# Weights of a float32 layer: rounded by the transfer, low parts made by a negative copy and an adding transfer

## The chip, the cores and the metric

The kernel runs on one core of a Trainium2 chip. The metric is the time of one execution on the device in microseconds (us). The engines that matter here are TensorE (PE: matmuls; its weight loads are listed as PEld), VectorE (DVE), ScalarE (ACT), GpSimd (POOL), which does almost no arithmetic here but issues some transfers, and SyncE (SP), which issues the rest. Every engine works through its own instructions in order.

## The reference

One decoder layer on 512 tokens of width 1024, all float32. Cut to what matters:

```python
h = rmsnorm(x, norm_mix_g)
proj = h @ w_in            # qk_ml, v_ml, o_ml, if, q_sw, k_sw, v_sw, g_a, g_b
h_ml = mlstm_chunkwise(q_ml, k_ml, v_ml, ig, lf)      # 4 heads
y_a  = sigmoid(o_ml) * norm(h_ml) * mlstm_norm_g
y_b  = swa_with_sinks(q_sw, k_sw, v_sw, sinks)        # window 128, 16 heads on 4
merged = sigmoid(g_a) * (y_a @ w_branch_a) + sigmoid(g_b) * (y_b @ w_branch_b)
x = x + merged @ w_out
x = x + square(relu(rmsnorm(x, norm_mlp_g) @ w_up)) @ w_down       # 1024 -> 4096 -> 1024
x = x + sigmoid(rmsnorm(x, norm_ple_g) @ w_ple_gate) * (p @ w_ple_proj)
return rmsnorm(x, final_norm_g)
```

The result must be right to float32 accuracy.

## The kernel before

**Products.** TensorE multiplies numbers of a rounded type, float32r. Each float32 operand is therefore split in two, a high part (the value rounded to float32r) and a low part (what is left, value − high), and a product is three matmuls: high·high, high·low, low·high (`pairs`, L154; the matmul itself is L162). 128 x 128 blocks of one operand are held, up to 512 columns of the other stream past.

**Weight tiles.** Weights lie in HBM as tiles of 128 partitions x 1024 values, 512 KB. SP loads a raw tile into a buffer `wr` (`load_raw`, L141; the load is L143), ACT rounds it into `wh` (L134), and DVE subtracts `wh` from the raw values into `wl` (L135). There are four buffers of each kind (`WRB` = 4 and `WB` = 4), so a raw tile is loaded while earlier ones are still at work. With one tile of `w_o`, `w_up` and the like, TensorE makes 24 matmuls of 512 columns (8 blocks x 3). `w_vsif` alone has two tiles of 1056 (4 x 264).

**Schemes of seven half products.** The value projection (`w_vml`), the two gates (`w_gb`, `w_ga`) and the down projection of the MLP (`w_down`) are written by Strassen-like schemes: seven products of half-sized blocks for eight. There DVE adds and subtracts raw weight tiles first, and the sums are split; each such tile feeds 12 matmuls of 512 columns or 24 of 256.

**Order of the work.** normalisation of x and `w_vsif` with it; `w_ksw` (2 tiles); `w_o` (8, among mLSTM gate arithmetic); the value scheme; the gates' schemes; then `w_qsw` and `w_qkml` (8 each), laid between the units of sliding-window attention; the mLSTM with `w_b` (8) between its heads; `w_a` (8); `w_out` (8); four rounds of up (8 tiles of `w_up`) and down (a scheme of 14 products); the projection of p (`w_pp`, 2); the gate projection (`w_pg`). `w_pg` is done in two halves: four tiles one after the other, each for all tokens, into four banks (psp); then, from L1073, four tiles that are all used for every 256 columns of every group of 128 tokens (psg), so that all four are needed within the first 48 matmuls. `gate` (L1029 to L1034) evicts: a sigmoid on ACT, a product and a sum on DVE, a square on ACT.

The tile framework puts each engine's instructions in an order of its own making when the program is built, and a buffer is reused when its last reader is through. POOL's queue held 16 stores of intermediate results to DRAM (`god<-sgo`, `gd<-gr`), 8 additions (L803) and the constants of the start.

Of the kernel before, what the change touches and what calls it, by code (L numbers as in the profile page):

```python
# [10 lines left out]
F32 = mybir.dt.float32  # L11
F32R = mybir.dt.float32r
AF = mybir.ActivationFunctionType
# [23 lines left out]
def block_kernel(  # L37
# [48 lines left out]
    def nm(s):  # L86
        n_names[0] += 1
        return f"{s}_{n_names[0]}"
# [50 lines left out]


    def load_raw(src, n):  # L141
        raw = wp.tile([P, 1056], F32, tag="wr", bufs=WRB, name=nm("wr"))
        nc.sync.dma_start(out=raw[:, :n], in_=src)  # L143
        return raw

    def load_w(src, n, dims, raw=None):

        if raw is None:
            raw = load_raw(src, n)
        parts = [wp.tile([P, 1056], F32R, tag=t, bufs=WB, name=nm(t))[:, :n] for t in ("wh", "wl")]  # L150
        split(parts, raw[:, :n])
        return [q.rearrange("p (k c) -> p k c", k=dims) for q in parts]

    def pairs(a, b):  # L154

# [8 lines left out]
    def quads(src, tags):  # L164

        t = []
        for i in range(len(tags)):
            if tags[i] == "wr":
                raw = wp.tile([P, 1056], F32, tag="wr", bufs=WRB, name=nm("wr"))[:, :1024]
            else:  # L170
                raw = sp.tile([P, 1024], F32, tag=tags[i], bufs=LMB if tags[i] == "lm" else 2, name=nm("wq"))
            nc.sync.dma_start(out=raw, in_=src[i])
            t.append(raw)
        return t
# [8 lines left out]
    def mm_tok(ps, w, acts, m, first=True, last=True):  # L183

        ops = []
        for k in range(len(acts)):
            ops += pairs([q[:, m * P : (m + 1) * P] for q in acts[k]], [q[:, k, :] for q in w])
        chain(ps, ops, first, last)
# [39 lines left out]
    nc.sync.dma_start(out=grow, in_=g_mix)  # L228
    load_x(0, 2)
    load_x(1)  # L230
    wv = [load_raw(w_vsif[c], 4 * 264) for c in range(2)]
    load_x(2)
    load_x(3)
    gml = cols(g_ml, KT, "gml", c1)
# [30 lines left out]
    for m in range(NT):  # L265
        xn = tok_scratch("xn")
        ss = small("ss", 1)
        A.activation(xn, xt[m], AF.Square, accum_out=ss)
        rs = rstd_of(ss, D)
        for c in range(2):  # L270
            o = slice(c * 512, (c + 1) * 512)
            V.scalar_tensor_tensor(xn[:, o], xt[m][:, o], rs, gmix[:, o], ALU.mult, ALU.mult)
        xns.append(xn)
        if m == 0:
            wv = [load_w(None, 4 * 264, 4, wv[c]) for c in range(2)]

    vs = []
    gt = c1.tile([P, NT, 8], F32, name="gt")
# [2 lines left out]
    for m in range(NT):  # L281
        for kq in range(2):
            ps = ps_t()
            for k in range(4):
                T.transpose(ps[:, k * P : (k + 1) * P], xns[m][:, kq * 512 + k * P : kq * 512 + (k + 1) * P], ident)
            split(
                [t[:, 4 * kq : 4 * kq + 4, m * P : (m + 1) * P] for t in h2],
                ps.rearrange("p (k c) -> p k c", k=4),
            )

        ps = ps_g()
        for c in range(2):
            mm_tok(ps[:, :264], wv[c], hT[c * 4 : c * 4 + 4], m, first=c == 0, last=c == 1)
        t = sp.tile([P, 256], F32, tag="vs", bufs=4, name=nm("vs"))
        A.copy(t, ps[:, :256])
        gate_in = V.tensor_add(gt[:, m, :], ps[:, 256:264], bif)
        vs.append(t)
# [576 lines left out]
    def load_down(q):  # L874
        raws = []
        for c in range(8):
            if c < 6:
                t = np_.tile([P, 1024], F32, tag="wd", bufs=6, name=nm("wd"))
            else:
                t = wp.tile([P, 1056], F32, tag="wr", bufs=WRB, name=nm("wr"))[:, :1024]  # L880
            nc.sync.dma_start(out=t, in_=w_down[q * 8 + c])
            raws.append(t)
        return raws

    def up(q, uf):
        fs = None
        for f in range(8):
            ps = ps_g()
            mm_T(ps, load_w(w_up[q * 8 + f], KT * P, KT), x1)
            a = mp.tile([P, 512], F32, tag="rt", bufs=3, name=nm("rt"))  # L890
            V.scalar_tensor_tensor(a, ps, 0.0, rB, ALU.max, ALU.mult)  # L891
            if f % 2 == 0:
                fs = F()
            o = 2 * (f % 2)
            A.activation(fs[:, o : o + 2, :].rearrange("p a b -> p (a b)"), a, AF.Square)
            if f % 2:
                hl = [np_.tile([P, 7 * 256], F32R, tag="uf", bufs=8, name=nm("uf")) for _ in range(2)]

                cut = 3 * 256 if f == 7 else 0
                if cut:  # L900
                    split([t[:, :cut] for t in hl], fs[:, 1:4, :].rearrange("p a b -> p (a b)"))
                V.tensor_add(fs[:, S1, :], fs[:, A21, :], fs[:, A22, :])
                V.tensor_sub(fs[:, S3, :], fs[:, A11, :], fs[:, A21, :])
                V.tensor_sub(fs[:, S2, :], fs[:, S1, :], fs[:, A11, :])
                V.tensor_sub(fs[:, S4, :], fs[:, A12, :], fs[:, S2, :])  # L905
                split([t[:, cut:] for t in hl], fs[:, 1 + cut // 256 :, :].rearrange("p a b -> p (a b)"))
                uf.append(hl)
# [221 lines left out]
def _layout(i):  # L1129
    w = i["w_in"][0]  # L1130
    down = i["w_down"][0]
    return {
        "x": i["x"][0],
        "p": i["p"][0, 0],
        "w_qkml": _t_form(w[:, 0:1024]),
        "w_vml": _quarters(w[:, 1024:2048]).reshape(2, 4, P, 1024).transpose(1, 0, 2, 3).reshape(8, P, 1024),
        "w_o": _t_form(w[:, 2048:3072]),
        "w_vsif": _tok_form(np.concatenate([w[:, 4360:4616], w[:, 3072:3080]], axis=1), 4, 264),
        "w_qsw": _t_form(_heads(w[:, 3080:4104])),
        "w_ksw": _t_form(w[:, 4104:4360]),  # L1140
        "w_ga": _halves(w[:, 4616:5640]),
        "w_gb": _halves(w[:, 5640:6664]),
        "w_a": _t_form(i["w_branch_a"][0]),
        "w_b": _t_form(_heads(i["w_branch_b"][0].T).T),
        "w_out": _tok_form(i["w_out"][0], 2, 512),
        "w_up": _t_form(i["w_up"][0]),
        "w_down": np.concatenate([_quarters(down[q * 1024 : (q + 1) * 1024]) for q in range(4)], axis=0),
        "w_pg": _tok_form(i["w_ple_gate"][0], 2, 512),
        "w_pp": _tok_form(i["w_ple_proj"][0], 2, 512),
        "g_mix": i["norm_mix_g"],  # L1150
        "g_ml": _columns(i["mlstm_norm_g"][0]),
        "g_mlp": _columns(i["norm_mlp_g"][0]),
        "g_ple": _columns(i["norm_ple_g"][0]),
        "g_fin": i["final_norm_g"][None, :],
        "conv": i["conv_qk"][0].reshape(4, KT, P).transpose(2, 1, 0).reshape(P, KT * 4),
        "b_if": i["b_if"],
        "sinks": i["sinks"],
    }
# [19 lines left out]
```

## Time and profile before

| | us |
|---|---|
| median of 3 runs | 921.12 (921.03 to 921.82) |
| profiled execution, span | 919.4 |
| PE busy | 903.5 (98%) |
| DVE busy | 646.0 (70%) |
| ACT busy | 448.5 (49%) |
| POOL busy | 23.4 (3%) |

The runs lie 1.7 us above the span of the profiled execution. In the profile a row of a group gives the line of the kernel, the engine, the operation, output tile <- input tiles with their shapes, the count, then the busy time, the mean duration of one in nanoseconds, and the engine's idle time before these instructions with what ended it. In the timeline a row is: start, duration, engine, line, operation, tiles, count, and in brackets the idle time before with its releaser. A row of the transfers: destination <- source, the queue, the count, KB each, and the median time in us from issue to landing. A row of the windows: the stretch, its length, then busy time (and number of instructions) of PE, PEld, DVE, ACT and POOL, the granted TensorE clock, the share of the transfer engines, GB/s. The rows themselves stand in the prediction.

### The profile page before, as it was taken

To read this page: it belongs to the slowest core of one execution; us is meant where nothing else is said; L and a number is where in the kernel's file an instruction comes from. 1 tells how busy PE (TensorE), PEld (TensorE's weight loads), DVE (VectorE), ACT (ScalarE), POOL (GpSimd) and SP (SyncE) were. 2 spreads that over 40 slices of the span, in tenths; PEclk is the share of its full clock that TensorE was granted. 3 is DMA by queue.
4 is the path that set the end of the run, shared out by engine and by line. 5 is a ranking of instruction groups with operands and counts; after the bars stand their busy time and mean duration, and the time that the engine had idled before them with its cause. 6 is when DMAs were issued, how large, how long until landed. Compare 5 with 4: busy or idle time off the path is not lost.

```text
span 919.4 us, 11810 instructions
## 1 busy us (share of the span) xinstructions
PE 903.5 (98%) x4524; PEld 743.6 (81%) x4524; DVE 646.0 (70%) x1026; ACT 448.5 (49%) x756; POOL 23.4 (3%) x41
## 2 busy tenths in 40 slices
PE   8999999999999999999999999999999999999996
PEld 6877889998777676778888888888888888888886
DVE  5776677874787877467653578757966895798556
ACT  6364444443676667564322545334434433454743
POOL 1001000000000000000210000000000000000000
PEclk9999999999999999999999999999999999999998
DMA  6643124434211132233452520631162044102302
GB/s 240 216 142 126 58 73 163 169 118 167 69 60 56 46 115 70 73 110 138 160 184 92 206 91 1 204 117 46 65 209 94 1 159 143 65 24 72 135 1 92
DMA packets 29851, 100.46 MB, mean 109 GB/s; under 512 B 4193, under 2 KB 4705, under 8 KB 29794
## 3 DMA queue, kind: packets, MB, share of 16 engines
q1 hardware_dynamic: 28002, 93.41, 29.6%
q0 software_dynamic: 1792, 6.29, 1.9%
q8 instruction: 35, 0.57, 0.3%
q14 instruction: 22, 0.18, 0.1%
HBM read 90.26 MB, written 8.39 MB: 107 GB/s over the span
## 4 chain that ended last, share of the span: by engine, by line
PE 74%; ACT 3%; DVE 2%; issue 0%; ACTq 0%
PE psg L162 41%; PE psp L162 23%; PE pst L736 2%; PE pst L663 1%; PE psa L655 1%; PE pst L726 1%; PE psa L162 1%; PE psa L618 1%; PE psp L829 1%; PE psa L619 1%; ACT jk L748 1%; ACT pT L657 0%; DVE it L1047 0%; PE psa L705 0%; ACT sgp L1034 0%
## 5 line engine op out<-in xcount | busy, mean ns | idle before, releaser
L134 ACT CAST wh<-wr 128x1024 fp32r<-128x1024 f32 (+1 forms) x136 | 142.4, 1050 | 211.5 <-PE psg L162 92.9
L135 DVE TENSOR_TENSOR wl<-wr,wh 128x1024 fp32r<-128x1024 f32 (+1 forms) x136 | 173.6, 1279 | 98.0 <-ACT wh L134 98.0
L162 PE MATMUL psg<-x,wh 128*128 128x512 f32 x512 | 159.9, 393 | 0.0
L162 PE MATMUL psp<-wh,uf 128*128 128x512 f32 x448 | 140.7, 393 | 0.0
L162 PEld LDWEIGHTS psg<-x,wh 128*128 128x128 f32 x512 | 96.3, 188 | 21.0
L162 PE MATMUL psg<-h,wh 128*128 128x512 f32 x320 | 101.8, 397 | 0.0
L162 PE MATMUL psg<-x,wl 128*128 128x512 f32 x256 | 100.5, 392 | 0.0
L162 PEld LDWEIGHTS psp<-wh,uf 128*128 128x128 f32 x448 | 84.1, 188 | 18.8
L162 PE MATMUL psp<-wl,uf 128*128 128x512 f32 x224 | 88.0, 393 | 0.0
L134 ACT CAST wh<-wd 128x1024 fp32r<-128x1024 f32 x44 | 46.2, 1052 | 60.7 <-PE psp L162 27.5
L162 PEld LDWEIGHTS psg<-h,wh 128*128 128x128 f32 x320 | 58.8, 188 | 16.2 <-issue 4.9
L162 PE MATMUL psg<-h,wl 128*128 128x512 f32 x160 | 63.2, 395 | 0.0
L135 DVE TENSOR_TENSOR wl<-wd,wh 128x1024 fp32r<-128x1024 f32 x44 | 53.6, 1221 | 5.2 <-ACT wh L134 5.2
L162 PEld LDWEIGHTS psg<-x,wl 128*128 128x128 f32 x256 | 48.1, 188 | 10.6
L162 PE MATMUL psa<-h,wh 128*128 128x256 f32 (+1 forms) x256 | 55.2, 312 | 0.6 <-ACT p L543 0.4
L162 PEld LDWEIGHTS psp<-wl,uf 128*128 128x128 f32 x224 | 42.1, 188 | 9.5
L135 DVE TENSOR_TENSOR uf<-F,uf 128x1792 fp32r<-128x1792 f32 (+2 forms) x20 | 33.0, 1651 | 21.8 <-ACT uf L134 21.8
L162 PEld LDWEIGHTS psa<-h,wh 128*128 128x128 f32 x256 | 41.6, 189 | 4.6 <-ACT p L543 1.3
L162 PE MATMUL psg<-yb,wh 128*128 128x512 f32 x128 | 42.6, 409 | 0.0
L891 DVE SCALAR_TENSOR_TENSOR rt<-psg,rB 128x512 f32<-128x512 f32 x32 | 22.0, 688 | 27.9 <-PE psg L162 27.9
L162 PE MATMUL psg<-ya,wh 128*128 128x512 f32 x128 | 40.8, 396 | 0.0
L134 ACT CAST uf<-F 128x1792 fp32r<-128x1792 f32 (+2 forms) x20 | 27.9, 1396 | 26.1 <-DVE F L905 26.0
(272 smaller groups left out, 1683.8 us busy)
## 6 DMA issues: line engine op xcount, KB each, us to landing
wr<-in_w_up SPq DMA_DIRECT2D x32, 512.0 KB, 3.3
wd<-in_w_down SPq DMA_DIRECT2D x24, 512.0 KB, 3.5
wr<-in_w_o SPq DMA_DIRECT2D x8, 512.0 KB, 4.1
gd<-gr POOLq DMA_DIRECT2D x8, 512.0 KB, 3.3
wr<-in_w_qsw SPq DMA_DIRECT2D x8, 512.0 KB, 4.3
wr<-in_w_qkml SPq DMA_DIRECT2D x8, 512.0 KB, 3.2
wr<-in_w_b SPq DMA_DIRECT2D x8, 512.0 KB, 3.2
gl<-gd SPq DMA_DIRECT2D x8, 512.0 KB, 3.2
```

The lines of the kernel that those rows point to most:

```text
L134: A.copy(dst[0], src)
L135: V.tensor_sub(dst[1], src, r32(dst[0]))
L162: last_mm[0] = T.matmul(ps, l, r, start=first and i == 0, stop=last and i == len(ops) - 1, skip_group_check=parts)
L618: T.matmul(o, q[:, n * P : (n + 1) * P], kk[kp][ab][:, k0 : k0 + 256], start=True, stop=False)
L619: T.matmul(o, q[:, n * P : (n + 1) * P], kl[kp][ab][:, k0 : k0 + 256], start=False, stop=True)
L655: T.transpose(pt[:, c : c + P], lm3[ab][:, g, j * P : (j + 1) * P], ident)
L663: T.matmul(o[HALF[ab], :], vs[n + 1 - nk + j][:, c : c + 64], pTs[j][:, ab * 512 : (ab + 1) * 512], start=j == 0, stop=j == nk - 1,)
L726: T.matmul(psc[:, n0:], qk[4 + h][:, n0 : n0 + P], qk[h][:, n0:], start=True, stop=True)
L736: T.matmul(pn[:, : DV + 1], wT[s][:, t * P : (t + 1) * P], vm[s][:, h, :], start=s == 0, stop=s == t)
L748: A.activation(jk[:, :DV], h_of(h, t), AF.Square, scale=rd[:, t : t + 1], accum_out=hss[:, h, t : t + 1])
L829: T.transpose(ps[:, m * P : (m + 1) * P], xk[m][:, k * P : (k + 1) * P], ident)
L891: V.scalar_tensor_tensor(a, ps, 0.0, rB, ALU.max, ALU.mult)
```

## The change

A second way to bring a weight tile in, `load_c`. POOL issues a transfer from HBM straight into `wh` that rounds on its way; ACT writes −`wh` into `wl`; POOL issues a second transfer of the same weights that adds them to what stands in `wl`, which leaves value − high there. No raw tile is needed, SP issues nothing for it and DVE does nothing. All weights take this way (92 tiles) but those of the schemes and `w_vsif`, which keep SP's load and the split by ACT and DVE. Tiles of all three kinds are now 1024 wide, and `w_vsif` comes in three (3, 3 and 2 blocks of 264 columns).

```diff
     def load_raw(src, n):
-        raw = wp.tile([P, 1056], F32, tag="wr", bufs=WRB, name=nm("wr"))
+        raw = wp.tile([P, 1024], F32, tag="wr", bufs=WRB, name=nm("wr"))
         nc.sync.dma_start(out=raw[:, :n], in_=src)
         return raw
 
     def load_w(src, n, dims, raw=None):
 
         if raw is None:
-            raw = load_raw(src, n)
-        parts = [wp.tile([P, 1056], F32R, tag=t, bufs=WB, name=nm(t))[:, :n] for t in ("wh", "wl")]
+            return load_c(src, n, dims)
+        parts = [wp.tile([P, 1024], F32R, tag=t, bufs=WB, name=nm(t))[:, :n] for t in ("wh", "wl")]
         split(parts, raw[:, :n])
         return [q.rearrange("p (k c) -> p k c", k=dims) for q in parts]
+
+    def load_c(src, n, dims):
+
+        hi, lo = [wp.tile([P, 1024], F32R, tag=t, bufs=WB, name=nm(t))[:, :n] for t in ("wh", "wl")]
+        G.dma_start(out=hi, in_=src)
+        A.activation(lo, r32(hi), AF.Copy, scale=-1.0)
+        G.dma_start(out=lo, in_=src, accum_op=ALU.add)
+        return [q.rearrange("p (k c) -> p k c", k=dims) for q in (hi, lo)]
...
-    wv = [load_raw(w_vsif[c], 4 * 264) for c in range(2)]
+    vsif = [(0, 3), (3, 3), (6, 2)]
+    wv = [load_raw(w_vsif[0, :, k0 * 264 : (k0 + n) * 264], n * 264) for k0, n in vsif]
...
-            wv = [load_w(None, 4 * 264, 4, wv[c]) for c in range(2)]
+            wv = [load_w(None, n * 264, n, raw) for (_, n), raw in zip(vsif, wv)]
...
-        for c in range(2):
-            mm_tok(ps[:, :264], wv[c], hT[c * 4 : c * 4 + 4], m, first=c == 0, last=c == 1)
+        for (k0, n), w in zip(vsif, wv):
+            mm_tok(ps[:, :264], w, hT[k0 : k0 + n], m, first=k0 == 0, last=k0 == 6)
...
-            mm_T(ps, load_w(w_up[q * 8 + f], KT * P, KT), x1)
+            mm_T(ps, load_c(w_up[q * 8 + f], KT * P, KT), x1)
```

The lines move by a few: the split is L134 and L135 in both, the new transfers are L157 (into `wh`) and L159 (adding, into `wl`), the negative copy L158.

How the instructions move is shown at three places. **The start**, SP's transfers before (loads of raw tiles):

```order
L143 DMA wr_364<-in_w_ksw 128x1024
L143 DMA wr_407<-in_w_ksw 128x1024
L143 DMA wr_503<-in_w_o 128x1024
L143 DMA wr_537<-in_w_o 128x1024
L143 DMA wr_624<-in_w_o 128x1024
```

and POOL's of the change, directly behind its constants, where before nothing stood until the first store of `sgo`:

```order
L157 DMA wh_370<-in_w_ksw 128x1024
L159 DMA wl_371<-in_w_ksw 128x1024
L157 DMA wh_412<-in_w_ksw 128x1024
L157 DMA wh_507<-in_w_o 128x1024
L157 DMA wh_540<-in_w_o 128x1024
L159 DMA wl_413<-in_w_ksw 128x1024
L159 DMA wl_508<-in_w_o 128x1024
L159 DMA wl_541<-in_w_o 128x1024
```

The loads have gone from SP to POOL, each tile twice. `wh_370` takes the one free buffer of four; the next three take those of the three tiles of `w_vsif`. On ACT the copies for these three now stand ahead of the casts of the keys (`kk`):

```order
L304 COPY vs_366<-psg_341 128x256
L158 ACTIVATE wl_413<-wh_412 128x1024
L158 ACTIVATE wl_508<-wh_507 128x1024
L158 ACTIVATE wl_541<-wh_540 128x1024
L323 CAST kk_399<-pst_369 64x512
```

**The output projection** `w_out`. POOL's queue of the change:

```order
L157 DMA wh_4512<-in_w_out 128x1024
L159 DMA wl_4513<-in_w_out 128x1024
L157 DMA wh_4541<-in_w_out 128x1024
L159 DMA wl_4542<-in_w_out 128x1024
L157 DMA wh_4570<-in_w_out 128x1024
L157 DMA wh_4599<-in_w_out 128x1024
L159 DMA wl_4571<-in_w_out 128x1024
L159 DMA wl_4600<-in_w_out 128x1024
```

Load and adding transfer alternate, so a tile's load stands behind the adding transfer of the tile before it, which stands behind ACT's copy of that tile; before, SP's queue held the raw loads alone.

**The second half of the gate projection** `w_pg`. POOL's last transfers of the change:

```order
L157 DMA wh_7321<-in_w_pg 128x1024
L157 DMA wh_7326<-in_w_pg 128x1024
L159 DMA wl_7322<-in_w_pg 128x1024
L159 DMA wl_7327<-in_w_pg 128x1024
L157 DMA wh_7331<-in_w_pg 128x1024
L157 DMA wh_7336<-in_w_pg 128x1024
L159 DMA wl_7332<-in_w_pg 128x1024
L159 DMA wl_7337<-in_w_pg 128x1024
```

and ACT's work there, of the change:

```order
L1038 ACTIVATE sgp_7289<-psp_7171,rs_7148 128x512
L158 ACTIVATE wl_7332<-wh_7331 128x1024
L1038 ACTIVATE sgp_7297<-psp_7171,rs_7155 128x512
L1043 ACTIVATE sgp_7289,fs<-xk 128x512
L1038 ACTIVATE sgp_7305<-psp_7172,rs_7162 128x512
L1038 ACTIVATE sgp_7313<-psp_7172,rs_7169 128x512
L1043 ACTIVATE sgp_7297,fs<-xk 128x512
L158 ACTIVATE wl_7337<-wh_7336 128x1024
```

The third tile's adding transfer has come behind the fourth tile's load, and the fourth tile's copy behind four sigmoids and two squares; before, the last cast (`wh_7423`) stood behind two sigmoids, and the raw tile was on chip.

More of the change, by code (lines that the diff above doesn't have):

```diff
@@ L168, in quads @@
             if tags[i] == "wr":
-                raw = wp.tile([P, 1056], F32, tag="wr", bufs=WRB, name=nm("wr"))[:, :1024]
+                raw = wp.tile([P, 1024], F32, tag="wr", bufs=WRB, name=nm("wr"))[:, :1024]
             else:
@@ L879, in load_down @@
             else:
-                t = wp.tile([P, 1056], F32, tag="wr", bufs=WRB, name=nm("wr"))[:, :1024]
+                t = wp.tile([P, 1024], F32, tag="wr", bufs=WRB, name=nm("wr"))[:, :1024]
             nc.sync.dma_start(out=t, in_=w_down[q * 8 + c])
@@ L1137, in _layout @@
         "w_o": _t_form(w[:, 2048:3072]),
-        "w_vsif": _tok_form(np.concatenate([w[:, 4360:4616], w[:, 3072:3080]], axis=1), 4, 264),
+        "w_vsif": _tok_form(np.concatenate([w[:, 4360:4616], w[:, 3072:3080]], axis=1), 8, 264),
         "w_qsw": _t_form(_heads(w[:, 3080:4104])),
```

## The prediction

> **What bounds the kernel now.** The page first: engine line and chain of waits.
>
> ```profile
> span 919.4 us, 11810 instructions
> PE 903.5 (98%) x4524; PEld 743.6 (81%) x4524; DVE 646.0 (70%) x1026; ACT 448.5 (49%) x756; POOL 23.4 (3%) x41
> PE 74%; ACT 3%; DVE 2%; issue 0%; ACTq 0%
> ```
>
> TensorE is busy for 98% of the span, and the chain that ended last runs along it. The change leaves all its products in place, so the end moves by what PE's waits gain or lose. The waits of PE, all of them by releaser:
>
> ```profile
> PE psa L655 <- ACT pT L657: 1.6, 1, 1.6
> PE psg L162 <- DVE h L135: 1.5, 4, 0.9
> PE psa L247 <- DVE eps_t L198: 1.1, 1, 1.1
> PE psg L162 <- ACT h L134: 1.1, 4, 0.4
> PE psg L162 <- DVE wl L135: 0.4, 1, 0.4
> PE psa L162 <- ACT p L543: 0.4, 1, 0.4
> PE pst L736 <- DVE hd L740: 0.2, 1, 0.2
> ```
>
> Of these 6.3 us only one, 0.4 us, is a wait for a low half of a weight, and the waits on L247 and on h belong to the start, where x arrives. So little can be won, and every new wait for a weight is lost in full. How much lead the weights have is read from the pace of the products, in the windows view:
>
> ```profile
> core 0: us, PE busy (x) PEld busy (x) DVE busy (x) ACT busy (x) POOL busy (x), PEclk, DMA share, GB/s
> 161.00:184.00 23.00, 23.00 (x193) 22.82 (x193) 18.80 (x23) 11.08 (x13) 1.06 (x2) 1.00 0.47 168
> 552.00:575.00 23.00, 23.00 (x102) 18.76 (x101) 20.11 (x24) 12.81 (x14) 0.00 (x0) 1.00 0.00 1
> ```
>
> At full clock a 512-column matmul takes 23.00/102 = 0.2255 us and a 256-column one 23.00/193 = 0.119 us. A full weight tile (24 products) lasts 5.41 us; a tile of a seven-half-product scheme (12 products) 2.71 us. There are four buffers per half, so a buffer that PE leaves is needed again three tiles later: after 16.2 us inside a run of full tiles, after 8.1 us where the three in between belong to a scheme.
>
> **The change, part by part.** What a tile costs today, and what a transfer takes, from the groups of the page, its transfers and queues, and POOL's timeline:
>
> ```profile
> L135 DVE TENSOR_TENSOR wl<-wr,wh 128x1024 fp32r<-128x1024 f32 (+1 forms) x136 | 173.6, 1279 | 98.0 <-ACT wh L134 98.0
> L134 ACT CAST wh<-wr 128x1024 fp32r<-128x1024 f32 (+1 forms) x136 | 142.4, 1050 | 211.5 <-PE psg L162 92.9
> wr<-in_w_up SPq DMA_DIRECT2D x32, 512.0 KB, 3.3
> gd<-gr POOLq DMA_DIRECT2D x8, 512.0 KB, 3.3
> q1 hardware_dynamic: 28002, 93.41, 29.6%
> 149.39 0.54 POOL L559 DMA_DIRECT2D gd<-gr  x1 [57.18 <-ACT gr L554]
> ```
>
> For 92 of these tiles the change removes one SP load and one DVE subtraction (92 x 1.28 = 118 us of DVE). ACT keeps one pass, now a copy with scale -1 in place of the cast; I take its 1.05 us. It adds 184 transfers on POOL, at 0.54 us of issue about 99 us of a POOL that is idle for 97%. None of this engine time lies on the path; the latency does. Today the raw tile lies ready, and a freed buffer is full again after 1.05 + 1.28 = 2.3 us. Now the rounding load starts only when PE has left the buffer: 3.3 us to landing, as for the plain transfers of both queues, then the copy at 1.05, then the adding transfer.
>
> The adding transfer is in no row. If it costs as a plain one, it lands after 3.3 us. All of q1's 93.41 MB took 29.6% of 919.4 us, 272 us, so 512 KB fill the engines for 1.5 us; if it reads both its sources one after the other, it needs 1.5 us more, and if it behaves like two whole transfers end to end, 6.6. I take 4.6, near the middle case, since it must move 512 KB from two places. The chain from a freed buffer is then 3.3 + 1.05 + 4.6 = 9.0 us (7.7 to 11). [...]
>
> So 9.0 us hide in 16.2 us and do not in 8.1. Beside that, two queues are in order: on POOL a low part's transfer waits for ACT's copy and holds back the next tile's rounding load; on ACT a copy that waits for its load holds back the evictions behind it. Place by place:
>
> *A, the start.*
>
> ```profile
> 31.98 0.62 PE L162 MATMUL pst<-h,wh 128*128 128x512 f32 x2
> 37.44 0.64 PE L162 MATMUL pst<-h,wh 128*128 128x512 f32 x2
> 11.85 1.60 SPq L143 DMA_DIRECT2D wr<-in_w_ksw  x2
> xt<-in_x SPq DMA_DIRECT2D x3, 512.0 KB, 8.3
> ```
>
> Before, both tiles of w_ksw were on chip by about 17 us. Now the second waits for the buffer of the first w_vsif tile, whose last product runs 15 matmuls of 264 columns before 31.98, near 30.1. Add 9.0: 39.1, against its need at 37.44, is 1.7 us. The first w_ksw tile is issued on POOL at about 4 us, among the loads of x that already take 8.3 us to land; one tile of 1.5 us ahead of them, to which the start is tied (the waits on h), makes 1.5 more, and the key casts behind the three copies a little: +3.5 (0, if no part of x is late and landings are quick, to 7, if the adding transfer costs 6.6 and both w_ksw transfers go ahead of x).
>
> *B, the projections behind the value scheme; D, w_b, w_a.* Each stretch of full tiles behind half-length ones begins with a border like F below, of 9.0 − 8.1 = 0.9 us; the copies that stand on ACT before the evictions of attention and branches add as much again: +2 each (0 to 6 and 0 to 8).
>
> *C, attention.* DVE loses the subtractions of w_qsw and w_qkml in and around it. What that can give back:
>
> ```profile
> 299.00:322.00 23.00, 21.28 (x114) 15.78 (x113) 20.67 (x73) 15.13 (x48) 0.00 (x0) 1.00 0.13 46
> 315.55 1.10 PE L655 MATMUL psa<-ident,lm 128*128 128x128 f32 x8 [1.58 <-ACT pT L657]
> ```
>
> In this stretch PE is busy for 21.28 of 23 us; with its neighbour some 2.7 us are idle, and DVE at 20.67 of 23 is why. I take −2 (−5.2, every wait of PE's table but L247's, to −1.6, the one wait).
>
> *E, w_out.* Eight full tiles, but on POOL load and low part alternate strictly (the piece of POOL's order stands with the change): the next load is issued behind the adding transfer, and its data go behind that transfer's on the same queue. One round is 4.6 + 1.5 + 1.05 = 7.2 us against 5.41 of products, 1.8 us a tile. Four tiles stand so: +7. If the two transfers overlap instead, a round is 0.54 + 3.3 + 1.05 = 4.9 and nothing is lost (0); with 6.6 a round is 9.2 and four tiles lose 14 with what the four loads of x (xk, in the same stretch) take.
>
> *F, three borders from down to up, and w_pp.* Three times 0.9, and the same for w_pp: +4 (0 if the landing is under 3.7 us; 8 with 6.6, less the queue's smoothing).
>
> *G, the gate projection at the end.*
>
> ```profile
> 887.21 0.39 PE L162 MATMUL psp<-wh,x 128*128 128x512 f32 x1
> 887.44 0.28 PE L162 MATMUL psg<-wh,x 128*128 128x256 f32 x1
> 890.29 0.40 PE L162 MATMUL psg<-wh,x 128*128 128x256 f32 x2
> 885.50 0.68 ACT L1029 ACTIVATE sgp<-psp,rs 128x512 f32<-128x512 f32 x1
> 887.64 1.05 ACT L134 CAST wh<-wr 128x1024 fp32r<-128x1024 f32 x1 [1.45 <-PE psp L162]
> 889.17 0.62 ACT L1034 ACTIVATE sgp<-xk 128x512 f32<-128x512 f32 x1
> 889.92 1.22 DVE L135 TENSOR_TENSOR wl<-wr,wh 128x1024 fp32r<-128x1024 f32 x1
> ```
>
> The second half begins at 887.44 and works 12 products on each of four tiles, 0.119 each. The low part of the third tile is needed at 890.3, that of the fourth at 891.7. On POOL the third low part now stands behind the fourth load, which can be issued only when the first half is over (887.4): its own issue falls at 888.15 and it lands at 892.75, a stall of 2.45. The fourth copy stands on ACT behind four sigmoids (0.68) and two squares (0.62 and a read-out) and ends near 892; its transfer is issued by 892.5 and lands at 897.1, against 894.2 with the first stall in: 2.9 more. Together they are the fourth's landing less its need without stalls, 892.5 − 891.7 + 4.6 = +5.4 (4.1 with 3.3, 7.4 with 6.6). No cover hides this, since four tiles are used up in 5.7 us.
>
> The rest of the run (w_o, w_qkml, up inside its runs) I cost at nothing: 9.0 hides in 16.2 us; without that cover each tile would lose 3.6. The narrower w_vsif tiles cost nothing: same columns, three casts for two.
>
> Sum: 3.5 + 2 + 2 − 2 + 7 + 4 + 5.4 = **+22**. On the profiled execution 919.4 + 22 = 941.4; the runs lie 1.7 us above it (median 921.12), so **943 us**. All low bounds give 919.4 − 5.2 + 4.1 = 918.3, so 920 us in runs; all high ones 919.4 + 7 + 6 + 8 − 1.6 + 14 + 8 + 7.4 = 968.2, so 970.
>
> **Rivals.** *First: the transfers become the bound, slower still.* A tile of 5.41 us must then carry a load of 1.5 us and an addition. With an addition of 3.9 us or more of all engines, or with the rounding load itself at double price, the queue's own pace, no longer PE, sets every full tile. At 5.41 + 0.9 us, 92 tiles lose 83 us: 1005. For it: no row shows an adding or converting transfer. Against it: POOL's plain ones land like SP's, 3.3 us. *Second: faster.* The new transfers land sooner than POOL's 256 KB ones,
>
> ```profile
> god<-sgo POOLq DMA_DIRECT2D x8, 256.0 KB, 2.6
> ```
>
> say after 2.0 us, so that a chain of 5.1 is under 8.1 at every border; only the tail loses (0.8 + 2.0 = 2.8), while attention and start give back all of 5.2: 921.1 − 2.4 = 918.7. It decides from landings under 2.3 us. For it: DVE is relieved where it is fullest. Against it: 512 KB land in no less than 3.2 us in any row of the list. *Third: no change.* Landings of 3.3 for both and no loss by alternation; the tail's 4.1 and the gain of 2.7 to 5.2 nearly cancel: 920.0 to 922.5.
>
> **How the numbers follow.** What a measurement of this kernel can tell from no change is 0.2%, 1.8 us. The forecast gets 0.57, the first rival 0.24, the second 0.07, the third 0.12. So faster 0.07, same 0.12, slower 0.81. The forecast's own range is 923 to 970, above the third rival and up to the high bounds. The range for 8 in 10 reaches down over the third rival to 920 and up to the first one's 1005.
>
> **What would show it.** In the list of transfers the landing of the adding ones (4.6) and of the rounding ones (3.3), the software queue's share rising from below 2% to 30–50%; DVE busy down by about 115 us; in PE's waits new ones for weights at the start near 37 us, in w_out and two at the second half of the gate projection (2.5 and 2.9 us), and the one at 315 us gone. If the waits sit inside the runs of full tiles as well, the first rival holds. The sum would be wrong with a landing under 3 us, or waits that ACT's evictions cause and no weight.

## The result, and the profile after

The changed kernel takes **1020.26 us** (median of four runs, 1013.05 to 1021.82) against 921.12: 1.106 times as long, with a 95% interval of 1.102 to 1.109. The forecast was 943, its range 920 to 1005. The direction was right; the size was more than four times the predicted 22 us.

The page after: span, engines, queues, and the transfers of one stage.

```profile
span 1019.0 us, 11893 instructions
PE 931.5 (91%) x4524; PEld 765.4 (75%) x4524; DVE 536.2 (53%) x935; ACT 448.3 (44%) x757; POOL 153.9 (15%) x225
q0 software_dynamic: 28288, 102.77, 43.9%
q1 hardware_dynamic: 14898, 45.17, 13.3%
wh<-in_w_up POOLq DMA_DIRECT2D x32, 512.0 KB, 6.1
wl<-in_w_up POOLq DMA_DIRECT2D x32, 512.0 KB, 5.4
```

TensorE makes the same 4524 matmuls, yet its busy time has risen from 903.5 to 931.5 us and its idle time from 15.9 to 87.5. DVE is 110 us lighter (118 were worked out). An adding transfer lands after 5.4 us (forecast 4.6), a rounding one after 6.1 (forecast 3.3). PE's largest waits now:

```profile
PE psp L838 <- DVE x L138: 13.4, 3, 6.3
PE psg L170 <- DMA wl<-in_w_up: 8.7, 3, 3.4
PE psg L170 <- DMA wl<-in_w_pg: 7.0, 3, 4.9
PE psp L170 <- DMA wl<-in_w_out: 5.7, 1, 5.7
PE psa L627 <- DVE qs L592: 5.0, 1, 5.0
PE psg L170 <- DMA wl<-in_w_o: 4.2, 1, 4.2
PE pst L170 <- DMA wl<-in_w_ksw: 3.6, 1, 3.6
```

Each weight for which the sum had a term has a wait for its low part (w_up, w_pg, w_out, w_ksw), but the largest row is no weight: PE waits 13.4 us for the split of x1, which ACT and DVE evict. That is one of the signs by which the prediction said its sum would be wrong, "waits that ACT's evictions cause and no weight". With the matmuls of both traces paired in order, the start of the same product gives the loss by stretch (us; stretches by the time in the kernel before; at 360 the two orders differ a little, so that about 1 us could stand on either side):

| stretch before | what runs | forecast | measured |
|---|---|---|---|
| 0 to 80 | w_vsif, w_ksw, w_o (A) | 3.5 | 18.9 |
| 80 to 211 | schemes of value and gates | 0 | −0.2 |
| 211 to 360 | w_qsw, w_qkml, attention (B, C) | 0 | 14.4 |
| 360 to 476 | w_b, w_a (D) | 2 | 9.2 |
| 476 to 545 | w_out, entry to up (E) | 7 | 24.4 |
| 545 to 866 | up and down, w_pp, first half of w_pg (F) | 4 | 20.3 |
| 866 to 910 | w_pg, second half (G) | 5.4 | 11.8 |
| | sum | 22 | 98.9 |

The rows are rounded. Where no weight comes the new way (80 to 211), nothing is lost.

### The profile page after: what moved, and what is told of

Read it like the earlier page. It is cut to its first block, busy times and chain, and to the rows that moved or that the text cites. A ratio compares the mean times of both kernels' runs of the same rounds, so it can differ in the third digit from the quotient of the medians.

```text
span 1019.0 us, 11893 instructions
## 1 busy us (share of the span) xinstructions
PE 931.5 (91%) x4524; PEld 765.4 (75%) x4524; DVE 536.2 (53%) x935; ACT 448.3 (44%) x757; POOL 153.9 (15%) x225
## 3 DMA queue, kind: packets, MB, share of 16 engines
q0 software_dynamic: 28288, 102.77, 43.9%
q1 hardware_dynamic: 14898, 45.17, 13.3%
## 4 chain that ended last, share of the span: by engine, by line
issue 38%; PE 33%; DMA 15%; POOL 5%; ACT 4%; DVE 4%; POOLq 0%; ACTq 0%; DVEq 0%
PE psg L170 23%; PE psa L170 5%; DMA wh<-in_w_up 3%; PE psp L170 2%; POOL wl L159 2%; DMA wh<-in_w_out 2%; POOL wh L157 2%; DMA wh<-in_w_b 2%; DMA wl<-in_w_up 2%; DMA wh<-in_w_o 2%; ACT wl L158 1%; DMA wh<-in_w_pg 1%; DVE wl L135 1%; PE pst L672 1%; DMA wr<-in_w_ga 1%
## 5 line engine op out<-in xcount | busy, mean ns | idle before, releaser
L158 ACT ACTIVATE wl<-wh 128x1024 fp32r<-128x1024 f32 x92 | 97.5, 1060 | 254.0 <-DMA wh<-in_w_up 98.5
L170 PE MATMUL psg<-x,wh 128*128 128x512 f32 x512 | 163.1, 400 | 0.0
L170 PEld LDWEIGHTS psg<-x,wh 128*128 128x128 f32 x512 | 99.3, 194 | 20.9
L170 PE MATMUL psg<-x,wl 128*128 128x512 f32 x256 | 103.0, 402 | 8.7 <-DMA wl<-in_w_up 8.7
L170 PE MATMUL psg<-h,wh 128*128 128x512 f32 x320 | 104.5, 406 | 0.0
L170 PEld LDWEIGHTS psg<-h,wh 128*128 128x128 f32 x320 | 61.2, 195 | 16.8 <-issue 4.3
L134 ACT CAST wh<-wr 128x1024 fp32r<-128x1024 f32 (+2 forms) x45 | 46.2, 1033 | 61.3 <-issue 20.4
L135 DVE TENSOR_TENSOR wl<-wr,wh 128x1024 fp32r<-128x1024 f32 (+2 forms) x45 | 53.6, 1199 | 36.3 <-ACT wh L134 36.3
L170 PE MATMUL psg<-h,wl 128*128 128x512 f32 x160 | 65.8, 411 | 7.3 <-DMA wl<-in_w_o 4.2
L134 ACT CAST wh<-wd 128x1024 fp32r<-128x1024 f32 x44 | 46.1, 1050 | 54.0 <-PE psp L170 19.8
L170 PEld LDWEIGHTS psg<-x,wl 128*128 128x128 f32 x256 | 50.0, 195 | 20.3 <-DMA wl<-in_w_up 9.9
L135 DVE TENSOR_TENSOR wl<-wd,wh 128x1024 fp32r<-128x1024 f32 x44 | 53.4, 1221 | 15.0 <-ACT wh L134 15.0
L157 POOL DMA_DIRECT2D wh<-in_w_up x32 | 22.6, 707 | 173.2 <-PE psp L170 133.6
L170 PEld LDWEIGHTS psg<-h,wl 128*128 128x128 f32 x160 | 31.4, 196 | 18.1 <-DMA wl<-in_w_o 4.7
L135 DVE TENSOR_TENSOR uf<-F,uf 128x1792 fp32r<-128x1792 f32 (+2 forms) x20 | 33.0, 1651 | 21.8 <-ACT uf L134 21.8
```

What stands on the lines that cost most here:

```text
L134: A.copy(dst[0], src)
L135: V.tensor_sub(dst[1], src, r32(dst[0]))
L157: G.dma_start(out=hi, in_=src)
L158: A.activation(lo, r32(hi), AF.Copy, scale=-1.0)
L170: last_mm[0] = T.matmul(ps, l, r, start=first and i == 0, stop=last and i == len(ops) - 1, skip_group_check=parts)
```

## The experiments

Each is one kernel with one profile and one time, beside the kernel before on the same chip (920.1 to 921.5 us); three, `v0_narrow`, `v1_aligned` and `v2_pool_sub`, were timed in several rounds. The four runs of the change itself spread over 9 us, so a single run that differs from it by less shows little by its time alone. Four theories were put on record. 1: the chain from a freed buffer to the low part, lengthened by POOL's order, is longer than its cover. 2: the transfer engines are full. 3: ACT, held by copies that wait for loads, evicts late. 4 came from the first runs: the place of the buffers.

### Narrow tiles without the new loading

This was the surprise, so it comes first. `e4_pool_plain` loads the 92 tiles raw by POOL, and ACT and DVE split them:

```diff
-        G.dma_start(out=hi, in_=src)
-        A.activation(lo, r32(hi), AF.Copy, scale=-1.0)
-        G.dma_start(out=lo, in_=src, accum_op=ALU.add)
+        raw = wp.tile([P, 1024], F32, tag="wr", ...)[:, :n]
+        G.dma_start(out=raw, in_=src)
+        split([hi, lo], raw)
```

> The 92 tiles are loaded raw, as before the change, but by POOL instead of SP; ACT rounds, DVE subtracts. Theory 1: raw tiles have buffers of their own and are loaded ahead, so POOL's queue as such costs nothing: 920 to 925 us. If POOL's transfers as such are slower or collide with DVE: 930 or more.

Measured: 917.47 us. POOL's queue as such costs nothing, as theory 1 had it, but neither expectation had a kernel *faster* than before. Over the whole run its products went a little quicker, about 0.5 us in 40. So SP's loading was put back, which leaves of the change only the widths and `w_vsif` in three (`e6_narrow_only`: `raw = load_raw(src, n)[:, :n]` and `split([hi, lo], raw)`, and the same kernel timed again as `v0_narrow`), and then a tile of 128 bytes was put ahead of all weight buffers (`e8_shift`):

```diff
+    pad = wp.tile([P, 32], F32, name="pad")
+    nc.vector.memset(pad, 0.0)
```

> The change without its new way of loading: tiles 1024 wide, w_vsif in three, all weights by SP, ACT and DVE as before. Theory 4 (in the kernel before, two of the four buffers of each half begin 32 bytes past a multiple of 256, the other two 160, and products with the first kind run at 232 ns, the others at 227; with a width of 1024 all are alike): as in the run with plain loads by POOL, 917 us, 7 us gained by the pace and 3 lost at the start. If POOL's plain loads had been what made that run faster: 921 to 924.

> The run with narrow tiles alone, and a tile of 128 bytes ahead of all weight buffers, which moves these and nearly all other tiles by 128 bytes, so that all begin 32 bytes past a multiple of 256. If the place itself is what matters, all products run at 232 ns and more: 930 to 940 us. If only the distance to the other operand matters, all are alike and fast: 917 us.

> The run with narrow tiles alone once more, timed: all weights by SP, ACT and DVE, tiles 1024 wide, w_vsif in three. Theory 4 (the distance of a weight tile to the other operand): 914 to 916 us, 0.7% faster than the kernel before.

Measured: 914.68, 915.02, and 916.08 in four runs (0.9948 of the kernel before, 0.993 to 0.9967). In the kernel before the two halves of a weight lie in buffers of 1056 values, 4224 bytes; two of four begin 160 bytes past a multiple of 256, like the activations, and two 32 bytes past one. Paired with the addresses of the built program, products of 512 columns with a weight of the first kind start 227 ns apart, with the second kind 232 to 233. In the kernel before, eight products of one tile of w_up and eight of a later one (the rows between left out) take 1.87 and 1.82 us:

```profile
541.17 0.40 PE L162 MATMUL psg<-x,wh 128*128 128x512 f32 x1
...
543.04 0.40 PE L162 MATMUL psg<-x,wh 128*128 128x512 f32 x1
```

```profile
546.73 0.39 PE L162 MATMUL psg<-x,wh 128*128 128x512 f32 x1
...
548.55 0.39 PE L162 MATMUL psg<-x,wh 128*128 128x512 f32 x1
```

Moved all together (`e8_shift`, 915.02 us), they are all fast: in these runs the pace goes with the distance of the two operands, not with the place. No other distance than 128 bytes modulo 256 was tried. The proof without `w_vsif` in three and without the width of 1024 is the kernel before with 1088 (4352 bytes, 17 x 256):

```diff
-        parts = [wp.tile([P, 1056], F32R, tag=t, bufs=WB, ...
+        parts = [wp.tile([P, 1088], F32R, tag=t, bufs=WB, ...
...
-    sel_f = c1.tile([4, 4, P], F32, name="sel_f")
+    sel_f = act_f("sel_f")[:4, :].rearrange("p (a b) -> p a b", a=4)
```

> The kernel before with weight halves 1088 wide in place of 1056 (w_vsif still in two tiles; the raw tiles stay 1056; the constant sel_f moves into a buffer of the activations to make room). Nothing but the width of the buffers speaks to the products. Theory 4: all buffers then lie at the same distance modulo 256 bytes from the other operand, 913 to 916 us as with 1024. If it is the width of 1024, or w_vsif in three tiles, that helps: 920 to 922.

Measured: **915.32 us**, 0.9938 of the kernel before (0.9923 to 0.9952), runs from 914.87 to 915.91. This version beats both kernels. The same window, nearly all four rounds of up and down, of the kernel before and of `v1_aligned` (columns as in the windows of the prediction):

```profile
526.00:850.00 324.00, 324.00 (x1414) 264.78 (x1413) 250.20 (x271) 139.35 (x147) 0.00 (x0) 1.00 0.28 93
```

```profile
526.00:850.00 324.00, 324.00 (x1442) 268.00 (x1441) 252.28 (x274) 143.41 (x153) 0.00 (x0) 1.00 0.30 98
```

At full clock and without a wait in both, 1442 products fit where 1414 did. Of the 28 more, 16 are short ones of 128 columns that the shift brings in at the window's end. The same 1413 products take 319.5 us in place of 324.0, 1.4% less; in `e8_shift` 319.7. `w_vsif` in three tiles, by contrast, brings a wait of its own: in `e6_narrow_only` one of 2.5 us for the split of h behind three subtractions, where the kernel before has 0.9.

```profile
PE psg L169 <- DVE h L135: 3.1, 4, 2.5
```

So the change held a gain of some 6 us, and its new way of loading costs 1019.0 − 913.0 = 106 us of span, not 99.6. The runs below are read against the narrow kernel's 915 to 916 us.

### Parts of the new loading

`e1_round_only` takes only the rounding load, `e2_add_only` only copy and adding transfer, `e3_no_add` keeps everything but the addition (it leaves the sum out, so its low parts hold other numbers):

```diff
 e1:   raw = load_raw(src, n)[:, :n]
       G.dma_start(out=hi, in_=src)
+      V.tensor_sub(lo, raw, r32(hi))
 e2:   raw = load_raw(src, n)[:, :n]
+      A.copy(hi, raw)
       A.activation(lo, r32(hi), AF.Copy, scale=-1.0)
       G.dma_start(out=lo, in_=src, accum_op=ALU.add)
 e3:   G.dma_start(out=hi, in_=src)
       A.activation(lo, r32(hi), AF.Copy, scale=-1.0)
-      G.dma_start(out=lo, in_=src, accum_op=ALU.add)
+      G.dma_start(out=lo, in_=src)
```

> High parts come by POOL's rounding transfer, low parts as before the change: SP loads the raw tile ahead, DVE subtracts. No negative copy, no adding transfer. Theory 1 (the chain from a freed buffer to the low part, lengthened by POOL's in-order queue, is longer than the cover): the chain is 3.5 + 1.3 = 4.8 us, under 8.1 at every border, and nothing on POOL waits for ACT, so nearly all of the 99 us go: 921 to 928 us. Theory 2 (the transfer engines, not the chain, are too full): each tile still takes two transfers of 512 KB, about 3 us of all engines, against 3.9 with the adding one; then only part of the loss goes: 950 to 990 us.

> High parts as before the change (SP's raw load ahead, ACT's cast), low parts by ACT's negative copy and POOL's adding transfer; DVE does nothing for them. Theory 1: the chain is 1.05 + 1.05 + 0.5 + 5.35 = 8.0 us, just the 8.1 of a border, and no rounding load stands behind an adding transfer: 925 to 940 us, with 6 us or so lost at the end of the gate projection. Theory 2: the engines carry 1.5 + 2.5 us per tile as in the change: 990 us or more. Theory 3 (ACT, held by copies that wait for loads, is late with evictions): copies no longer wait for loads, so it too expects under 950.

> The change, with a second rounding load in place of the adding transfer: the low part then holds the rounded weight, so the low products are left as they are but of other numbers, and the sum of value and negative copy is left out. Queue, waits and bytes are those of the change. Theory 1: the second transfer lands after 3.5 in place of 5.35 us and the load behind it 1 us or more sooner, a round of POOL is about 6.5 us in place of 8.1: about half of the loss goes, 950 to 975 us. If the double time of the addition were all of it: under 935. If it were nothing (queue order alone): over 990.

Measured: 933.26, 953.16 and 957.85 us: 18, 38 and 42 over the narrow kernel, where both together with the addition cost 105. Theory 2's 950 to 990 and over 990 are missed by far in the first two, though both still move every tile twice; theory 1's 921 to 928 and 925 to 940 are missed by 5 and 13, and theory 3's "under 950" for the second by 3. Only the third fell where theory 1 put it. It shows that 62 of the 105 us hang on the adding transfer's longer time. That time lengthens the chain and fills the engines at once, so this run does not tell the two theories apart. The parts do not add up, 18 + 38 against 105; a likely reason, which no run separates, is that they share one cover and one queue, and what one uses up the other lacks. `e3` also gives the price of a rounding load to the engines:

```profile
q0 software_dynamic: 28288, 102.77, 34.1%
wh<-in_w_up POOLq DMA_DIRECT2D x32, 512.0 KB, 4.6
wl<-in_w_up POOLq DMA_DIRECT2D x32, 512.0 KB, 3.9
```

34.1% of its span of 956.2 us, less 17.5 for POOL's stores (1.9% of 919.4, before), is 308.6 us for 184 transfers, 1.68 each. In the change the same sum is 430 us for 92 pairs, 4.67 a pair, so an adding transfer takes 2.99 us of all engines, 1.8 times a rounding one. Why, no run here shows.

### The engine that makes the copy

```diff
-        A.activation(lo, r32(hi), AF.Copy, scale=-1.0)
+        V.tensor_scalar_mul(lo, r32(hi), -1.0)
```

> The change with the negative copy on DVE in place of ACT; nothing else differs. Theory 3 (ACT, held by copies that wait for their loads, is late with evictions: the two waits of 6.3 and 6.2 us for the split of x1, and others): ACT's evictions are free again, 985 to 1005 us, unless DVE, which takes half of each split, is held in the same way. Theory 1 (chain and POOL's order): the chain is as long as before, 1010 to 1025 us.

Measured: 1048.27 us, worse by 28 and above both ranges. Up to 440 us, in `w_a`, it was 11 us ahead of the change, then it lost 39. Its waits:

```profile
PE psp L838 <- DVE xk L856: 18.5, 4, 9.8
PE psg L170 <- DMA wl<-in_w_pg: 16.7, 4, 6.1
PE psg L170 <- DVE rt L900: 13.2, 5, 4.7
```

The wait for the split of x1 (13.4 in the change) is down to 1.3, and in its place stand DVE's evictions of `xk` and `rt`. The chain is as long as in the change: from the issue of the rounding load to the landing of the low part the median of the 92 tiles is 13.0 us in both. Theory 3's mechanism is shown by that, its number is not: whichever engine makes the copy holds its evictions back, and here DVE's cost more than ACT's.

### POOL's order

`e7_lead` and `e9_lead_late` issue the next tile's rounding load ahead of this tile's adding transfer:

```diff
+        nxt = load_hi(ahead, n)      # G.dma_start into the next tile's wh, kept in program order
         A.activation(lo, r32(hi), AF.Copy, scale=-1.0)
         G.dma_start(out=lo, in_=src, accum_op=ALU.add)   # kept in program order
```

> The change with one alteration of order in w_a, w_out, w_up and w_pg: on POOL the rounding load of the next tile is issued ahead of the adding transfer of this one. Buffers, bytes and engines are those of the change. Theory 1: in the alternating stretches a round of 8.1 us falls under 5.41, while the borders from down to up and the end of the gate projection keep most of their stalls; of the some 60 us lost from w_a on (433 us in the profile before) a third to a half goes: 985 to 1000 us. Theory 2 (the transfer engines are full): no change, 1015 or more.

> The change, with the next tile's rounding load ahead of this tile's adding transfer on POOL in w_up and w_pg alone; up to w_out POOL's order is that of the change, so no store and no addition is moved behind a transfer. Theory 1: from 540 us of the profile before to its end the change loses 32 us; the same stretch lost 15 in the run that had this order everywhere. So 1000 to 1008 us. If the gain of that stretch came from elsewhere: 1018 or more.

Measured: 1191.87 and 1010.99 us. The first lost through its own construction: transfers held in program order also stand in order with POOL's stores and additions, so in `w_o` a tile's transfers wait behind a store, and in `w_a` behind an addition, that waits for the tile before:

```profile
632.59 1.26 POOL L822 TENSOR_TENSOR sga<-sga,gb 128x512 f32<-128x512 f32 x1 [14.67 <-DVE sga L821]
633.80 0.59 POOL L156 DMA_DIRECT2D wh<-in_w_a  x1
634.38 0.91 POOL L165 DMA_DIRECT2D wl<-in_w_a  x1
649.37 1.26 POOL L822 TENSOR_TENSOR sga<-sga,gb 128x512 f32<-128x512 f32 x1 [14.08 <-DVE sga L821]
```

That is one tile in 16.8 us in place of 5.4, the price of an in-order queue in its plainest form. `e9`, which leaves these alone, gives back 9 us, less than the 12 to 20 expected and no more than the spread of the change's own runs. By the paired traces most of it (7 us) comes in the entry to up, where one stall of 6 us is gone; the borders stay. So in w_up and w_pg POOL's order is a small part. For `w_out`, where load and low part alternate, `e9` says nothing, and `e7`, which has the new order there too, points the other way: from 476 to 545 us of the kernel before it loses 3.1 us, the change 24.4. Just before, PE had stood 12 us for the first tile of w_out, which lets POOL run ahead, so that is no proof; whether POOL's order is the larger part of the loss in w_out and the entry stays open. `e7` also has the three borders' waits (9.0 us, the change 8.7), yet from 545 to 866 it loses 9.7 us in place of 20.3.

### The borders from down to up

`e10_up_only` uses the new loading for `w_up` alone; `e11_up_covered` adds one buffer for each half, for the first tile of every round.

```diff
 e10, e11: (load_w, no raw tile given)
-            return load_c(src, n, dims)
+            raw = load_raw(src, n)
 e11:
+    xw = pool(st_m, "xw")
-            mm_T(ps, load_c(w_up[q * 8 + f], KT * P, KT), x1)
+            mm_T(ps, load_c(w_up[q * 8 + f], KT * P, KT, xw if f < 1 else None), x1)
```

> The new way of loading for the 32 tiles of w_up alone; all other weights by SP, ACT and DVE in narrow tiles. The kernel with narrow tiles alone takes 915 to 916 us. Theory 1 (each border from a scheme to full tiles costs the chain of 10.5 us less its cover of 8.1, and what the lowered clock adds behind the stall): the three borders lost 6.1, 4.6 and 5.7 us in the change, and the first round begins behind tiles that still come early: 16 to 22 us, 932 to 938 us. If the stages disturb each other (late evictions and transfers of one stage delay the next), the borders alone cost less: under 926.

> The run before this one, with one further buffer for each half, used by the first tile of every round of up, so that this tile is loaded during the round before and the second tile has 8.1 + 5.4 = 13.5 us for its chain of 10.5. Theory 1 (cover, not amount of transfers, decides): the borders' stalls go, 916 to 922 us. Theory 2 (the transfers as such, or POOL's order, cost the time): as without the buffer, 930 or more.

Measured: 947.43 and 940.76 us. `e10` is over its range, with losses of 6.4, 6.3 and 6.6 us at the three borders and 7 at the entry. `e11` has no loss left at the borders: the waits for low parts of w_up fall from the first row to the second.

```profile
PE psg L170 <- DMA wl<-in_w_up: 10.9, 3, 3.8
```

```profile
PE psg L171 <- DMA wl<-in_w_up: 3.9, 3, 1.9
PE psg L171 <- DVE rt L902: 3.2, 2, 2.3
PE psp L171 <- DVE p L956: 3.0, 2, 1.5
```

But behind the entry the run still loses 16 us against the narrow kernel, in place of 22, now inside the rounds, from the fourth tile on. So the total missed theory 1's 916 to 922 and fell where theory 2 put it, at 930 or more. The cover decides at the border, as theory 1 says; behind it the next limit waits, the pace at which POOL's queue brings tiles (below). Whether that pace is POOL's order or the engines' share, which reaches 0.9 and more in these stretches, was not told apart.

### Relief for DVE in attention

`v2_pool_sub` is the narrow kernel with POOL's subtraction (`G.tensor_tensor(lo, raw, r32(hi), ALU.subtract)`) for the 16 tiles of w_qsw and w_qkml.

> Narrow tiles alone, and POOL, idle there, does the subtraction of the 16 tiles of w_qsw and w_qkml in place of DVE. The term for attention in the prediction was -2 us for a relieved DVE (the wait of 1.6 us for pT and its neighbours). If that term holds: 912 to 914 us, 1 to 2 under the narrow kernel; if POOL's subtraction, at over 2 us, is too slow or hinders DVE: 916 or more.

Measured: 920.5 us (0.9989 of the kernel before, 0.9971 to 1.0006), 4 over the narrow kernel by the medians. PE's wait for `pT`, and what POOL and DVE did just before it:

```profile
PE psa L667 <- ACT pT L669: 2.4, 1, 2.4
```

```profile
311.19 3.03 POOL L160 TENSOR_TENSOR wl<-wr,wh 128x1024 fp32r<-128x1024 f32 x1 [8.09 <-ACT wh L159]
312.11 2.13 DVE L642 TENSOR_SCALAR nmx<-mx 128x4 f32<-128x4 f32 x1
```

The wait for `pT` grew from 1.6 to 2.4. But this run is no clean test: an operation of DVE on 4 values per partition, which takes 0.14 to 0.17 us in the kernel before, takes 2.13 us here and ends within 0.02 us of POOL's subtraction, which itself takes 3.03 us where the median of the 16 is 2.40. That is one place; it speaks for the second branch of the expectation, that POOL's subtraction hinders DVE. The cleaner test is `e2_add_only`, where no engine subtracts for these tiles: there the wait for `pT` is 1.1 us, and the stretch from 211 to 360 is no faster than in the narrow kernel. So the relief is worth some 0.5 us at that wait, and no run shows the −2 of the term C.

## Why the prediction was wrong, point by point

**Where the 106 us went.** The rows of PE's waits hold 34.9 us for parts of weights (the narrow kernel has none) and 42.3 us for work of ACT and DVE (9.0 in the narrow kernel); and the same products keep PE busy for 36 us longer. So there are three parts of about the same size, 35, 33 and 36 us. The sum had the first at 22 us, the second only within the +2 of B and of D, and the third not at all.

**What bounds the kernel** was right: every new wait for a weight is lost in full, and there was little to win. That the pace of the products was not one number was overlooked: "0.2255 us" came from 102 starts in one window, whose ends cut it, and the two paces of 227 and 232 ns stood in the timeline of before.

**The chain.** With nothing ahead of it a rounding load is in place 3.6 us after its issue at 558.41 (forecast 3.3), and one round of POOL can be read from three places:

```profile
558.41 0.55 POOL L157 DMA_DIRECT2D wh<-in_w_up  x1 [4.55 <-PE psg L170]
563.38 0.86 POOL L159 DMA_DIRECT2D wl<-in_w_up  x1 [4.42 <-ACT wl L158]
563.92 0.89 POOL L157 DMA_DIRECT2D wh<-in_w_up  x1
571.43 0.87 POOL L159 DMA_DIRECT2D wl<-in_w_up  x1 [6.62 <-ACT wl L158]
```

```profile
562.03 1.06 ACT L158 ACTIVATE wl<-wh 128x1024 fp32r<-128x1024 f32 x1 [8.75 <-DMA wh<-in_w_up]
570.08 1.06 ACT L158 ACTIVATE wl<-wh 128x1024 fp32r<-128x1024 f32 x1 [6.99 <-DMA wh<-in_w_up]
```

The load issued at 558.41 lets the copy start at 562.03. The next, issued 0.54 behind an adding transfer, only at 570.08, 6.2 later. In the change 35 rounding loads are issued within 0.7 us behind an adding transfer; each landed at least 1.24 us after that transfer, and 6.6 us after its own issue in the median. Then the adding transfer at 571.43: a round of 8.05 us (forecast 7.2). Alone the chain is 3.6 + 1.06 + 0.3 + 5.4 = 10.4 us, inside the bounds of 7.7 to 11; behind another tile's adding transfer it is 13. Over the 92 tiles, from the issue of the rounding load to the landing of the low part, the median is 13.0 us: 11 tiles keep within the upper bound of 11, and 11 need more than the 16.2 us of cover. The *mechanism* was right at its place; the step that failed is the size in "So 9.0 us hide in 16.2 us and do not in 8.1", with the round counted for four tiles of w_out alone. All stretches of full tiles go through that queue, and 13 us leave 3 for everything that ACT and POOL put ahead.

**A clock that was not priced.** The failed step here is the sum itself, which charged a stall at its own length. Behind the stall of 5.67 us for w_out the products run at half clock (PE's timeline, and the same stretch in the windows):

```profile
528.53 0.79 PE L170 MATMUL psp<-wl,mg 128*128 128x512 f32 x1 [5.67 <-DMA wl<-in_w_out]
529.13 1.05 PE L170 MATMUL psp<-wh,mg 128*128 128x512 f32 x2
529.98 0.63 PE L170 MATMUL psp<-wl,mg 128*128 128x512 f32 x1
```

```profile
528.00:532.00 4.00, 3.46 (x8) 2.79 (x9) 0.00 (x0) 0.00 (x0) 0.00 (x0) 0.50 0.97 252
532.00:536.00 4.00, 4.00 (x17) 3.18 (x16) 0.00 (x0) 1.06 (x1) 1.43 (x2) 0.86 0.26 23
```

0.425 us a product in place of 0.227, for some 4 us: 2 us more for a stall of 5.7. Over the run PE is busy 931.5 us in the change and 895.1 in the narrow kernel, with the same 4524 products, 36 us more; the other 70 of the 106 are waits. PE is busy for 64.1 us in the stretches granted half the clock, which accounts for **32 of these 36 us**, in the narrow kernel for none. In the change half clock comes with each of the 15 stalls of 2.1 us or more, for 3.41, 6.83 or 10.24 us by the clock's records, and with none of the four between 1.4 and 2.0. The length alone does not decide: the stall of 2.48 us for the split of h has it in the change (0.85 over the first 23 us) and not in `e6_narrow_only` (1.00). In the rounds of `e11`, whose stalls are at most 2.4 us, the stretch with the longest keeps a clock of 1.00:

```profile
630.00:635.00 5.00, 2.65 (x12) 1.89 (x11) 2.63 (x2) 1.73 (x4) 0.16 (x1) 1.00 0.90 274
```

**A (3.5, measured 18.9).** The wait for the second tile of w_ksw was named and is there, 3.6 us against 1.7. Not counted: the rounds of 8 to 10 us in the tiles of w_o behind it (4.2), half clock behind these stalls, and a clock of 0.85 in the first 23 us, where the narrow kernel had 0.93 to 1.00 and the kernel before 1.00. The last, some 3 us, is not shown to be the new loading's doing: `e4_pool_plain`, which has none of it, has 0.85 as well, and the narrow kernel 1.00 in one profile (`e6_narrow_only`) and 0.93 in the other (`v0_narrow`).

**B and C (0, measured 14.4).** The gain from DVE did not come (`e2_add_only`); the waits that came are for the evictions of q (5.0) and the low parts of w_qsw (3.0). The first is B's own step, an eviction behind a copy on ACT, at five times its price: ACT stood for a load while the casts of q (`qs`) waited behind the copy, and likewise later in D the work on `dm`:

```profile
261.02 1.06 ACT L158 ACTIVATE wl<-wh 128x1024 fp32r<-128x1024 f32 x1 [5.15 <-DMA wh<-in_w_qsw]
```

```profile
434.36 1.06 ACT L158 ACTIVATE wl<-wh 128x1024 fp32r<-128x1024 f32 x1 [4.29 <-DMA wh<-in_w_a]
```

**E (7, measured 24.4).** The alternation was right in kind: one stall of 5.7 for the low part. The larger share of the waits was a step that stood in the text of B and D only, evictions held on ACT by copies. This step failed by its size: 1 us for each of B and D, and nothing for E. Here it cost two stalls of over 6 us; one of them, in ACT's timeline and in PE's:

```profile
548.96 1.06 ACT L158 ACTIVATE wl<-wh 128x1024 fp32r<-128x1024 f32 x1 [7.48 <-DMA wh<-in_w_out]
549.92 1.83 ACT L137 ACTIVATE x<-psp,gmlp 128x512 fp32r<-128x512 f32 x3
```

```profile
551.43 1.11 PE L838 MATMUL psp<-ident,xk 128*128 128x128 f32 x4 [6.32 <-DVE x L138]
```

ACT waits 7.5 us for a load, the split of x1 stands behind it, PE behind that.

**F (4, measured 20.3).** The borders were named at 0.9 us each; they cost 6 (`e10`), the chain's overrun and the clock behind it. In the change the first tile of these rounds has its low part 10.5 to 11.6 us after the issue of its load, and PE stands 2.2 to 3.4 us there.

**G (5.4, measured 11.8).** The two stalls are there, for the third and the fourth low part, 4.9 and 0.95 us in place of 2.45 and 2.9, together 5.85 against 5.35; the third's and the fourth's transfer follow one another as worked out. Not foreseen were 1.2 us for the second low part and 0.5 for the third rounding load, which stand behind the first half's transfers, and the rest, some 4 us, is the products at half clock behind:

```profile
976.36 0.39 PE L170 MATMUL psg<-wl,x 128*128 128x256 f32 x1 [1.18 <-DMA wl<-in_w_pg]
977.68 0.51 PE L170 MATMUL psg<-wh,x 128*128 128x256 f32 x2 [0.46 <-DMA wh<-in_w_pg]
...
984.51 0.58 PE L170 MATMUL psg<-wl,x 128*128 128x256 f32 x1 [4.90 <-DMA wl<-in_w_pg]
...
988.39 0.58 PE L170 MATMUL psg<-wl,x 128*128 128x256 f32 x1 [0.95 <-DMA wl<-in_w_pg]
```

**D (2, measured 9.2)** is of B's kind: PE stood 2.2 us for `dm` and 3.3 for `sy`, both behind a copy that waited on ACT, with half clock after both. The run inside up was "costed at nothing", and in the change it is next to nothing once a round has begun with a stall; that the stall lets POOL run ahead is the likely reason, since `e11`, without it, loses inside the rounds.

**The rivals.** The first, at 1005, came nearest in time, but not by its condition: an adding transfer takes 3.0 us of all engines, not 3.9, a rounding one 1.7, and over the whole run the engines were busy for 57% (43.9 + 13.3). That its time came near is luck. The second and third fell with the landing of 5.4. The change does hold a gain, but in a place that no rival named: the width of the buffers.

## What to carry to other kernels

Here the transfers that replaced work of an engine were paid in latency, 13.0 us from issue to low part in the median where 2.3 us had refilled a buffer: count the whole chain from the moment that a buffer comes free, with the in-order queues it passes, against the time until the buffer is needed, in every stage and not only at the places where the order looks bad. Price a stall with the slow clock that may follow it (in the change it followed each from 2.15 us up). Ask of each engine that is to wait for a load what stands behind that wait in its queue. Read the pace of the products tile by tile: an even division over a window hides two populations.

## What the runs showed of the hardware that was not expected

- **The distance between a product's two operands went with its pace.** In the kernel before, with weight buffers 4224 bytes apart, two of four lie 128 bytes off the others modulo 256; products of 512 columns with these start 232 to 233 ns apart in place of 227. With 4096 bytes three start every 0.68 us (`e10_up_only`, 535 to 565 us). The same 1413 products that take 324.0 us in the kernel before take 319.5 with 4352 bytes (`v1_aligned`), and 319.7 with 4096 and the whole moved by 128 bytes (`e8_shift`). `v1_aligned` takes 0.9938 of the time of the kernel before.
- **An adding transfer** of 512 KB into SBUF lands after 5.4 us (median of w_up in the change) and takes 3.0 us of all engines, worked out from the queue shares of the change and of `e3`; a rounding one 3.6 us with nothing ahead of it, and 1.7. A rounding load issued right behind an adding transfer lands after 6.6 (median of 35 in the change).
- **Half clock after a stall**: 0.425 us a product for about 4 us behind the change's stall of 5.67. In the change it comes with every stall from 2.15 us up and with none up to 1.94; in `e6_narrow_only` it stays away after one of 2.48.
- **A DVE operation beside a subtraction of POOL.** In `v2_pool_sub` a DVE operation on 4 values per partition, 0.14 to 0.17 us in the kernel before, took 2.13 us and ended within 0.02 us of a subtraction of POOL.
